# Moving POOL's arithmetic to DVE, and a new order of layer 0's second MLP half

## The chip, the cores and the metric

The kernel runs on one core of one Trainium2 chip. The metric is the device time of one execution in microseconds. The engines in the profile are PE (TensorE matmuls; PEld its weight loads), DVE (VectorE), ACT (ScalarE), POOL (GpSimd) and SP (SyncE, which issues most DMAs). Each engine works through its own list of instructions in order; an instruction starts when what it needs has been signalled.

## The reference

A two-layer backbone over 1024 latent tokens and 256 context tokens, width 1024, in float32:

```python
def modulate(h, shift, scale):
    return h * (1 + scale) + shift

def sq_relu_mlp(h, w1, w2):
    return jnp.square(jax.nn.relu(h @ w1)) @ w2

# even layer: one projection -> [bidirectional chunked GLA | GQA with QK-RMSNorm and 2-D axial rotary]
y = jnp.concatenate([y_a, y_b], axis=-1) @ w_out
# odd layer: one projection -> [bidirectional order-2 Hyena | differential attention with rotary]
y = jnp.concatenate([hyena, diff], axis=-1) @ w_out
# both: pre-RMSNorm, adaLN shift and scale, mixer (or MLP), post-RMSNorm, adaLN gate, residual add
```

The context tokens pass through layer 0 whole; of layer 1 only the latent tokens are put out. The shift, scale and gate vectors come from the conditioning vector by six projections per layer.

## The kernel before

**Matmuls in three terms.** Each float32 operand is split into a high part, rounded to PE's format, and a low part, the rest. `split` (L92) has ACT copy `hi` (L94) and then DVE or POOL subtract `lo = src - hi` (L95); its flag `pool` says which. A product is then three matmuls: hi·hi, lo·hi, hi·lo.

**Stages.** Layer 0: the in-projection, with head norms (L488) and roping (`rope`, L606: L611 multiplies on DVE, L616 and L618 multiply and add on POOL) and, in the background, `ada_halves`, which works out modulation vectors on DVE (L259, L261) and splits the sums as `ada_hl`; grouped attention, woven with Hyena's filters (`hy_filters`, whose loads `hy_m` POOL issues); GLA (lines 875 to 1047; gating at L1004 and L1008, the decayed keys at L927, the masked scores at L960); the out-projection with its norms and residuals (`post_norm`, L1050, whose last add, L1061, alternates between POOL and DVE); and the MLP. Layer 1: the in-projection with short convolutions (`cb_hi`, `cb_lo`), differential attention (L644 to L668) woven with it, Hyena's long convolution (`hy_conv`, whose loads `hm` POOL issues, whose sums L1955 to L1961 DVE does), the out-projection (`wo_hi`, `wo_lo`) and the MLP.

**The MLP's first half** (`Up`) forms the seven products of a Strassen-like scheme, in 16 blocks of the hidden width, and writes the blocks to HBM as `hid`. Its weight splits `w_lo<-up_w` are shared by POOL and DVE; the flag `by_pool` of `keep` (L1208) says which.

**The second half** (`mlp_down`, L1414) has seven products too, in the order p1, p2, p3, p5, p6, p7, p4 (`DOWN`), each summed in PSUM over 16 blocks k of the hidden width: 112 steps. A step i has three parts. `load(i)` fetches a block of activations (`dn_h`) and one or two of weights (`dn_b`; `dn_t` for those that p5, p6 and p4 share), and, where context tokens take part, `dn_c`. `prep(i + 2)` subtracts weight blocks where the product asks for it (L1477) and splits both operands into pairs (`dn_h_hi`, `dn_h_lo`, `dn_w_hi`, `dn_w_lo`), then calls `load` for a step further on. `terms` issues twelve matmuls (L1515 to L1517) into four PSUM banks, `context` six more (L1526 to L1528) in p1, p2, p3 and p5. After a product's last block `put` (L1490 to L1500) adds the banks into the accumulators `accx` and `accy`. The context's sums `accz` are complete after p5, those of the first four row tiles of latent tokens (`accx`) after p7, the other four (`accy`) after p4. `ends` is a pipeline of stages (post-norm and residual, then the next layer's norm) that the program advances in every second step of p7 and p4, the context's tiles first; the scheduler puts the context's gating on DVE before p6's last splits. The modulation vectors that are still missing run beside the steps as `bg`, at the pace of `rates`. The tuple `bufs` gives the numbers of buffers: activations, weights, context blocks, pairs; it is (5, 6, 4, 6) in layer 0.

**What sets the order.** DMAs wait in order on the queue of the engine that issues them. Names of a buffer ring make a write wait until the last reader of that buffer is done. The order of each engine's list comes from a scheduler that follows the program's order and the waits between instructions, so a change of engine for one instruction also shifts its neighbours; tables below show the lists.

Of the kernel before, what the change touches and what calls it, by code (L numbers as in the profile page):

```python
# [91 lines left out]
def split(g, hi, lo, src, pool=False):  # L92

    g.nc.scalar.activation(hi, src, ACTF.Copy)  # L94
    (g.nc.gpsimd if pool else g.nc.vector).tensor_tensor(lo, src, f(hi), op=ALU.subtract)  # L95
# [369 lines left out]
def in_proj0(g, ps, ftp, vgp):  # L465
# [12 lines left out]
    with ExitStack() as st:  # L478
# [6 lines left out]
        def head_norm(src, nh, gain):  # L485
            r = head_rstd(g, pq[0], src, nh, 64, f"rp_u{nh}")
            nc.vector.tensor_tensor(src, src, r.unsqueeze(2).to_broadcast([128, nh, 64]), op=ALU.mult)
            nc.gpsimd.tensor_tensor(src, src, gain.unsqueeze(1).to_broadcast([128, nh, 64]), op=ALU.mult)  # L488
# [117 lines left out]
def rope(g, pool, src, nh, t1, t2):  # L606
# [8 lines left out]
    for k in range(2):  # L615
        nc.gpsimd.tensor_tensor(uv[:, :, :, k], sv[:, :, :, 1 - k],  # L616
                                tv[:, :, k].unsqueeze(1).to_broadcast([128, nh, 32]), op=ALU.mult)
    nc.gpsimd.tensor_tensor(o, o, u, op=ALU.add)  # L618
# [207 lines left out]
def gla(g, st, y_put):  # L826
# [81 lines left out]
    def weights(t, b, p, la):  # L908
# [18 lines left out]
        nc.gpsimd.tensor_tensor(gate(ee), gate(ee), kb, op=ALU.mult)  # L927
# [23 lines left out]
    def inner(t, b, ee, kinT):  # L951
# [8 lines left out]
        nc.gpsimd.tensor_tensor(aT, ab[b][:, :, 0, :], ab[b][:, :, 1, :], op=ALU.add)  # L960
# [31 lines left out]
    def forward(t):  # L992
# [11 lines left out]
        nc.gpsimd.tensor_scalar(sgf, gt, -80.0, None, op0=ALU.max)  # L1004
# [3 lines left out]
        nc.gpsimd.tensor_tensor(sgf, sgf, gt, op=ALU.mult)  # L1008
# [41 lines left out]
def post_norm(g, y, x_t, gate, tmp, junk, pool=True):  # L1050
# [10 lines left out]
    (nc.gpsimd if pool else nc.vector).tensor_tensor(x_t, x_t, tmp, op=ALU.add)  # L1061
# [116 lines left out]
class Up:  # L1178
# [235 lines left out]
def mlp_down(g, layer, ap, pool, x_src, bg, rates, after, group, bufs):  # L1414
# [25 lines left out]
    raws, parts, cs, gates = {}, {}, {}, []  # L1440
# [5 lines left out]
    def load(i):  # L1446
# [3 lines left out]
        q = nc.scalar if i < 2 else nc.sync  # L1450
# [81 lines left out]
    def tiles(n):  # L1532
        return [psa(g, [128, 512], name="dn_ps", tag="dp") for _ in range(n)]
# [17 lines left out]
    ends = [done(t, zs[t]) for t in range(len(zs))] + [done(NC_T + t, xs[t]) for t in range(4)]  # L1551
    ends = pipelined(item(e) for e in ends)
# [6 lines left out]
    for i, (n, k) in enumerate(steps[:len(steps) - group]):  # L1559
# [73 lines left out]
def w_block(g, raw, pool=None, split_pairs=False):  # L1633
# [4 lines left out]
    if split_pairs:  # L1638
        h, r = (x.rearrange("p k (c d) -> p (k c) d", d=64) for x in (hi, raw))
        l = lo.rearrange("p k (c d) -> p (k c) d", d=64)  # L1640
        for x in range(2):
# [3 lines left out]
            (nc.vector if 2 > x else nc.gpsimd).tensor_tensor(l[:, :, sl], v, f(h[:, :, sl]), op=ALU.subtract)  # L1645
# [728 lines left out]
def tile_kernel(ctx, tc, ins, out):  # L2374
# [57 lines left out]
    with st:  # L2432
        with ExitStack() as s2:
            ap, pool = pool_of(s2, "acc0", "left"), pool_of(s2, "res0", "left")
            hs = {}
            with ExitStack() as sp:
# [3 lines left out]
                                (norm, hs.__setitem__), 4, (5, 6, 4, 6))  # L2440
# [150 lines left out]
```

## Time and profile before

| | us |
|---|---|
| median of three runs (lowest, highest) | 3390.24 (3385.76, 3394.58) |
| the profiled execution, and its span | 3387.06, 3385.3 |
| PE busy | 3134.7 (93%) |
| DVE busy, 4507 instructions | 2489.5 (74%) |
| ACT busy | 1538.6 (45%) |
| POOL busy, 392 instructions | 528.0 (16%) |
| mean granted clock of TensorE | 0.967 of full speed |

The times in the prediction's rows are microseconds from the span's start. The stages lie about as follows: layer 0's in-projection to 345, attention to 690, GLA and the filters to 960, out-projection to 1115, the MLP's first half to 1464 and second half to 1900; layer 1's in-projection and attention to 2400, Hyena to 2645, out-projection to 2800, and its MLP to the end.

### The profile page before, as it was taken

The numbers are of one execution on the slowest core, as the hardware profiler recorded it, in microseconds if no ns is written. First come the engines' busy times: TensorE is split into PE (matmuls) and PEld (weight loads), VectorE is DVE, ScalarE is ACT, GpSimd is POOL, SyncE is SP. The second block draws the span as 40 slices with busy tenths as digits, with TensorE's granted clock in tenths as the row PEclk, the third lists the DMA queues.
The fourth block names the chain that finished last, engine by engine and source line by source line (L and its number), as shares of the span: only waits on it lengthen the run. The fifth ranks groups of instructions, "written<-read, shape, count | busy, mean of one in ns | idle before, by whom it ended". The sixth has DMA issues, their size and how long they took to land.

```text
span 3385.3 us, 41884 instructions
## 1 busy us (share of the span) xinstructions
PE 3134.7 (93%) x13896; PEld 2405.3 (71%) x13896; DVE 2489.5 (74%) x4507; ACT 1538.6 (45%) x3150; POOL 528.0 (16%) x392
## 2 busy tenths in 40 slices
PE   8879999889987999989998899999968989999998
PEld 4766777667766788868876777766635667887886
DVE  6787767677658776766688666677778489877777
ACT  4444766554655222223345543576621352224453
POOL 0153000123222122201111112100020122210000
PEclk9999999999998999999999999999989999999999
DMA  6544111667753343378777455432344635438964
GB/s 227 154 129 147 55 40 47 178 193 228 244 199 114 132 146 131 134 255 297 240 245 241 135 167 168 116 97 74 122 142 135 226 113 168 146 137 303 314 194 161
DMA packets 344581, 566.69 MB, mean 167 GB/s; under 512 B 43329, under 2 KB 138561, under 8 KB 344236
## 3 DMA queue, kind: packets, MB, share of 16 engines
q1 hardware_dynamic: 296244, 491.19, 44.4%
q10 hardware_dynamic: 40952, 47.67, 4.1%
q0 software_dynamic: 7168, 25.17, 2.5%
q8 instruction: 109, 1.79, 0.2%
q14 instruction: 108, 0.88, 0.1%
HBM read 410.36 MB, written 153.55 MB: 167 GB/s over the span
## 4 chain that ended last, share of the span: by engine, by line
PE 63%; DVE 14%; issue 10%; DMA 7%; ACT 3%; POOL 3%; SPq 0%; ACTq 0%; POOLq 0%; DVEq 0%
PE up_ps L105 5%; PE up_ps L104 5%; PE up_ps L103 5%; PE dn_ps L1516 5%; PE dn_ps L1515 5%; PE dn_ps L1517 5%; PE s_ps L644 2%; PE up_ps L1234 1%; PE s_ps L738 1%; PE o_ps L2224 1%; DMA up_w<-in_w_mlp_in 1%; PE st_ps L758 1%; PE st_ps L759 1%; DVE ada_acc L261 1%; PE o_ps L771 1%
## 5 line engine op out<-in xcount | busy, mean ns | idle before, releaser
L1515 PE MATMUL dn_ps<-dn_w_hi,dn_h_hi 128*128 128x512 f32 x896 | 351.3, 394 | 28.2 <-DVE accy L1496 14.3
L1516 PE MATMUL dn_ps<-dn_w_lo,dn_h_hi 128*128 128x512 f32 x896 | 352.9, 394 | 5.3 <-DVE dn_w_lo L95 5.3
L1517 PE MATMUL dn_ps<-dn_w_hi,dn_h_lo 128*128 128x512 f32 x896 | 351.5, 392 | 0.0
L94 ACT ACTIVATE dn_h_hi<-dn_h 128x512 fp32r<-128x512 f32 x224 | 140.8, 629 | 279.4 <-PE dn_ps L1516 192.1
L95 POOL TENSOR_TENSOR w_lo<-up_w,w_hi 128x512 fp32r<-128x512 f32 x106 | 144.4, 1372 | 582.8 <-ACT w_hi L94 548.1
L95 DVE TENSOR_TENSOR dn_h_lo<-dn_h,dn_h_hi 128x512 fp32r<-128x512 f32 x224 | 161.9, 723 | 83.7 <-ACT dn_h_hi L94 83.3
L1515 PEld LDWEIGHTS dn_ps<-dn_w_hi,dn_h_hi 128*128 128x128 f32 x896 | 169.8, 190 | 67.7 <-DVE accy L1496 16.1
L1516 PEld LDWEIGHTS dn_ps<-dn_w_lo,dn_h_hi 128*128 128x128 f32 x896 | 170.1, 190 | 43.6 <-DVE dn_w_lo L95 8.5
L1517 PEld LDWEIGHTS dn_ps<-dn_w_hi,dn_h_lo 128*128 128x128 f32 x896 | 170.1, 190 | 35.4
L261 DVE SCALAR_TENSOR_TENSOR ada_acc<-w_ada,sc,ada_acc 128x512 f32<-128x512 f32 x224 | 169.0, 791 | 19.7 <-DMA w_ada<-in_w_ada 19.0
L94 ACT ACTIVATE s_hi<-up_w 128x512 fp32r<-128x512 f32 x128 | 79.1, 630 | 192.6 <-DVE up_w L1223 113.3
L95 DVE TENSOR_TENSOR gq_lo<-gq_p,gq_hi 128x512 fp32r<-128x512 f32 x168 | 115.4, 690 | 55.9 <-ACT gq_hi L94 54.3
L105 PE MATMUL up_ps<-t_hi,s_lo 128*128 128x512 f32 x384 | 152.3, 398 | 2.4 <-DVE s_lo L95 2.4
L104 PE MATMUL up_ps<-t_lo,s_hi 128*128 128x512 f32 x384 | 152.0, 396 | 2.8 <-DVE t_lo L95 2.8
L103 PE MATMUL up_ps<-t_hi,s_hi 128*128 128x512 f32 x384 | 152.6, 397 | 1.4 <-ACT t_hi L94 1.3
L1223 DVE TENSOR_TENSOR up_w<-up_w 128x512 f32<-128x512 f32 x128 | 94.0, 737 | 79.0 <-POOL w_lo L95 77.2
L654 DVE TENSOR_REDUCE sm_m<-s_ps 128x1 f32<-128x512 f32 (+1 forms) x192 | 110.2, 595 | 44.7 <-PE s_ps L644 43.3
L95 POOL TENSOR_TENSOR ada_hl<-ada_acc,ada_hl 128x512 fp32r<-128x512 f32 x32 | 62.3, 1958 | 510.7 <-ACT ada_hl L94 359.4
L739 DVE TENSOR_REDUCE gq_mx<-s_ps 128x1 f32<-128x256 f32 (+1 forms) x208 | 112.2, 580 | 29.1 <-PE s_ps L738 28.2
L668 ACT ACTIVATE df_p<-s_ps,sm_m 128x512 f32<-128x512 f32 (+1 forms) x192 | 116.7, 618 | 34.5 <-DVE sm_m L658 31.1
L94 ACT ACTIVATE w_hi<-up_w 128x512 fp32r<-128x512 f32 x106 | 64.7, 628 | 142.4 <-DMA up_w<-in_w_mlp_in 63.5
L761 ACT ACTIVATE gq_p<-st_ps 128x512 f32<-128x512 f32 x168 | 99.7, 597 | 61.2 <-PE st_ps L759 60.3
(499 smaller groups left out, 8906.6 us busy)
## 6 DMA issues: line engine op xcount, KB each, us to landing
dn_b<-in_w_mlp_out SPq DMA_DIRECT2D x252, 256.0 KB
w_ada<-in_w_ada SPq DMA_DIRECT2D x96, 512.0 KB
up_w<-in_w_mlp_in SPq DMA_DIRECT2D x32, 1024.0 KB
hy_m<-in_k_ff POOLq DMA_DIRECT2D x32, 512.0 KB, 5.1
dn_c<-hidc SPq DMA_DIRECT2D x64, 256.0 KB
x<-x_in SPq DMA_DIRECT2D x26, 512.0 KB
x_in<-x SPq DMA_DIRECT2D x26, 512.0 KB
cb_raw<-in_od_w_in SPq DMA_DIRECT2D x20, 512.0 KB
```

Source lines behind the costliest of these rows:

```text
L94: g.nc.scalar.activation(hi, src, ACTF.Copy)
L95: (g.nc.gpsimd if pool else g.nc.vector).tensor_tensor(lo, src, f(hi), op=ALU.subtract)
L103: nc.tensor.matmul(out, ah, bh, start=(i == 0), stop=False)
L104: nc.tensor.matmul(out, ah, bl, start=False, stop=False)
L105: nc.tensor.matmul(out, al, bh, start=False, stop=(i == n - 1))
L261: nc.vector.scalar_tensor_tensor(acc[:, s], w[:, k], sc, acc[:, s], op0=ALU.mult, op1=ALU.add)
L654: nc.vector.tensor_reduce(m[:, i:i + 1], s, axis=AX.X, op=ALU.max)
L668: g.nc.scalar.activation(d, s, ACTF.Exp, bias=m, scale=0.125, accum_out=l[:, i:i + 1])
L739: nc.vector.tensor_reduce(mx[u][:, i, j:j + 1], ps, axis=AX.X, op=ALU.max)
L1515: nc.tensor.matmul(ps, hh[:, sl], wh, start=(k == 0), stop=False)
L1516: nc.tensor.matmul(ps, hh[:, sl], wl, start=False, stop=False)
L1517: nc.tensor.matmul(ps, hl[:, sl], wh, start=False, stop=(k == nb - 1))
```

## The change

It has two parts.

**The engine of arithmetic.** Every tensor operation that POOL did moves to DVE, but for the low parts of the weights in the MLP's first halves (`w_lo<-up_w`, 106 instructions): 212 instructions, 116 of them 512 elements wide, 40 of 1024, two of 2048, and 54 of 256 or less. `split` now ignores its fifth positional argument, so that only a call that names `pool=` reaches POOL. POOL keeps these w_lo, some fills of memory, and DMA issues.

**Layer 0's second MLP half.** The first two steps' loads are issued by POOL instead of ACT; activations and weights have 8 and 9 buffers instead of 5 and 6, the pairs 4 instead of 6; the `dn_t` tiles are taken from the pool of loads at the start; the context's gate is fetched at the start of p6 and the context's ends run there, in a pipeline of their own, while the latent tokens' ends stay in p7 and p4; of the four banks of p7 two come from the context's ring (`cx`), of those of p4 one, so that three of the four are not those that the product before holds to its end (before, all came from one ring of five, `dp`).

```diff
-def split(g, hi, lo, src, pool=False):
+def split(g, hi, lo, src, _=False, pool=False):
...
-                nc.gpsimd.tensor_tensor(lo, src, f(hi), op=ALU.subtract)
+                nc.vector.tensor_tensor(lo, src, f(hi), op=ALU.subtract)
...
-            nc.gpsimd.tensor_tensor(src, src, gain.unsqueeze(1).to_broadcast([128, nh, 64]), op=ALU.mult)
+            nc.vector.tensor_tensor(src, src, gain.unsqueeze(1).to_broadcast([128, nh, 64]), op=ALU.mult)
...
-        nc.gpsimd.tensor_tensor(uv[:, :, :, k], sv[:, :, :, 1 - k],
+        nc.vector.tensor_tensor(uv[:, :, :, k], sv[:, :, :, 1 - k],
...
-    nc.gpsimd.tensor_tensor(o, o, u, op=ALU.add)
+    nc.vector.tensor_tensor(o, o, u, op=ALU.add)
...
-        nc.gpsimd.tensor_tensor(gate(ee), gate(ee), kb, op=ALU.mult)
+        nc.vector.tensor_tensor(gate(ee), gate(ee), kb, op=ALU.mult)
...
-        nc.gpsimd.tensor_scalar(sgf, gt, -80.0, None, op0=ALU.max)
+        nc.vector.tensor_scalar(sgf, gt, -80.0, None, op0=ALU.max)
...
-        nc.gpsimd.tensor_tensor(sgf, sgf, gt, op=ALU.mult)
+        nc.vector.tensor_tensor(sgf, sgf, gt, op=ALU.mult)
...
-    (nc.gpsimd if pool else nc.vector).tensor_tensor(x_t, x_t, tmp, op=ALU.add)
+    nc.vector.tensor_tensor(x_t, x_t, tmp, op=ALU.add)
...
-        split(self.g, hi, lo, src, by_pool)
+        split(self.g, hi, lo, src, pool=by_pool)
...
-    raws, parts, cs, gates = {}, {}, {}, []
+    raws, parts, gates = {}, {}, {}
+    if ctx:
+        ts = {k: rp.tile([128, 512], F32, name=f"dn_t{k}") for k in range(nb)}
...
-        q = nc.scalar if i < 2 else nc.sync
+        q = (nc.gpsimd if ctx else nc.scalar) if i < 2 else nc.sync
...
-        return [psa(g, [128, 512], name="dn_ps", tag="dp") for _ in range(n)]
+        tags = {"p7": ("dp", "cx", "cx", "dp"), "p4": ("dp", "dp", "dp", "cx")} if ctx else {}
+        return [psa(g, [128, 512], name="dn_ps", tag=tag) for tag in tags.get(n, ("dp",) * 4)]
...
-    ends = [done(t, zs[t]) for t in range(len(zs))] + [done(NC_T + t, xs[t]) for t in range(4)]
-    ends = pipelined(item(e) for e in ends)
+    ctx_ends = pipelined(item(done(t, zs[t])) for t in range(len(zs)))
+    ends = pipelined(item(done(NC_T + t, xs[t])) for t in range(4))
...
+            if n == "p6" and ctx:
+                gates.update({1: mod(g, p, layer, 5, (1,), name="gate")[0]})
             if n == "p7":
                 run(bg)
-                gates.extend(mod(g, pool, layer, 5, range(2 - layer), name="gate", tag="gate", bufs=2))
+                gates.update({0: mod(g, pool, layer, 5, (0,), name="gate", tag="gate", bufs=2)[0]})
...
+        if n == "p6" and k % 2:
+            next(ctx_ends, None)
...
-                                (norm, hs.__setitem__), 4, (5, 6, 4, 6))
+                                (norm, hs.__setitem__), 4, (8, 9, 4, 4))
```

The lists of instructions below are as they are issued, without times; a row's names are out<-in, its sizes partitions x elements, and xN stands for N like rows in a row.

ACT at the end of layer 0's first MLP half, before (`up_r`, `up_c`: the last block's context rows; `hid_0p` and `hid_1p`: the first two blocks of activations):

```order
L1237 COPY up_r<-up_ps 128x256
L94 ACTIVATE up_c<-up_r 128x256
L1452 DMA dn_h<-hid_0p_9557 128x512
L1460 DMA dn_b<-in_w_mlp_out 128x512
L1452 DMA dn_h<-hid_1p_9564 128x512
L1460 DMA dn_b<-in_w_mlp_out 128x512
L94 ACTIVATE dn_h_hi<-dn_h 128x512
L94 ACTIVATE dn_w_hi<-dn_b 128x512
```

POOL with the change, at the same place of the program:

```order
L95 TENSOR_TENSOR w_lo<-up_w,w_hi 128x512 x64
L1454 DMA dn_h<-hid_0p_9557 128x512
L1464 DMA dn_b<-in_w_mlp_out 128x512
L1454 DMA dn_h<-hid_1p_9564 128x512
L1464 DMA dn_b<-in_w_mlp_out 128x512
L1990 DMA hm<-in_k_df 128x512 x8
```

The four issues left ACT's list, where they stood between the first half's last split and the second half's first, for POOL's, where they stand behind the last of layer 0's w_lo.

DVE in layer 0's second half, before, among the splits for p6's last two steps (`accz`: the context's sums; `dn_t`: p6's weights):

```order
L95 TENSOR_TENSOR dn_w_lo<-dn_t_16147,dn_w_hi 128x512
L1060 SCALAR_TENSOR_TENSOR accz_13914<-accz_13914,rs_t,gate 128x1024
L1060 SCALAR_TENSOR_TENSOR accz_13915<-accz_13915,rs_t,gate 128x1024
L95 TENSOR_TENSOR dn_h_lo<-dn_h,dn_h_hi 128x512
L95 TENSOR_TENSOR dn_w_lo<-dn_t_16186,dn_w_hi 128x512
L1061 TENSOR_TENSOR x_in<-x_in,accz_13915 128x1024
```

DVE with the change, among the splits for p6's steps 6 and 7:

```order
L1060 SCALAR_TENSOR_TENSOR accz_13914<-accz_13914,rs_t,gate 128x1024
L95 TENSOR_TENSOR dn_h_lo<-dn_h,dn_h_hi 128x512
L1061 TENSOR_TENSOR x_in<-x_in,accz_13914 128x1024
L95 TENSOR_TENSOR dn_w_lo<-dn_t_13928,dn_w_hi 128x512
L95 TENSOR_TENSOR dn_h_lo<-dn_h,dn_h_hi 128x512
L95 TENSOR_TENSOR dn_w_lo<-dn_t_13929,dn_w_hi 128x512
```

The gating of the context's sums moved forward by some eight steps, the two tiles stand apart, and both residual adds are now in DVE's list, one of which POOL had.

POOL at the end of Hyena's convolution, before (`hm`: the transform's matrices; `wo_lo`: the out-projection's weights):

```order
L1981 DMA hm<-in_k_df 128x512 x2
L95 TENSOR_TENSOR wo_lo_23224<-wo_raw,wo_hi_23223 128x1024
L1981 DMA hm<-in_k_di 128x512
L95 TENSOR_TENSOR wo_lo_23230<-wo_raw,wo_hi_23229 128x1024
L1981 DMA hm<-in_k_di 128x512
L95 TENSOR_TENSOR wo_lo_23236<-wo_raw,wo_hi_23235 128x1024
```

DVE with the change, there (`hz`: the convolution's outputs, from PSUM):

```order
L1970 TENSOR_TENSOR hz<-y_ps,hz 128x512 x2
L95 TENSOR_TENSOR wo_lo_23224<-wo_raw,wo_hi_23223 128x1024
L95 TENSOR_TENSOR wo_lo_23230<-wo_raw,wo_hi_23229 128x1024
L1970 TENSOR_TENSOR hz<-y_ps,hz 128x512 x2
L95 TENSOR_TENSOR wo_lo_23236<-wo_raw,wo_hi_23235 128x1024
L95 TENSOR_TENSOR wo_lo_23242<-wo_raw,wo_hi_23241 128x1024
```

The eight wo_lo left their places between POOL's DMA issues for places between DVE's evacuations.

More of the change, by code (lines that the diff above doesn't have):

```diff
@@ L959, in inner @@
         aT = wk.tile([128, 4, 128], F32, name="gl_aT", tag="gl_aT")
-        nc.gpsimd.tensor_tensor(aT, ab[b][:, :, 0, :], ab[b][:, :, 1, :], op=ALU.add)
+        nc.vector.tensor_tensor(aT, ab[b][:, :, 0, :], ab[b][:, :, 1, :], op=ALU.add)
         return t, b, ee, aT
@@ L1455, in load @@
             if n == "p5" and b == "b12":
-                w = ts[k] = p.tile([128, 512], F32, name=f"dn_t{k}")
+                if not ctx:
+                    ts[k] = p.tile([128, 512], F32, name=f"dn_t{k}")
+                w = ts[k]
             else:
@@ L1565, in mlp_down @@
         if k == 0:
-            ps = tiles(4)
+            ps = tiles(n)
             if n in ("p1", "p3") and ctx:
                 cps = [psa(g, [128, 512], name="dc_ps", tag="cx") for _ in range(2)]
+            if n == "p6" and ctx:
+                gates.update({1: mod(g, p, layer, 5, (1,), name="gate")[0]})
             if n == "p7":
                 run(bg)
-                gates.extend(mod(g, pool, layer, 5, range(2 - layer), name="gate", tag="gate", bufs=2))
+                gates.update({0: mod(g, pool, layer, 5, (0,), name="gate", tag="gate", bufs=2)[0]})
         for t in range(4):
@@ L1644, in w_block @@
             nc.scalar.activation(h[:, :, sl], v, ACTF.Copy)
-            (nc.vector if 2 > x else nc.gpsimd).tensor_tensor(l[:, :, sl], v, f(h[:, :, sl]), op=ALU.subtract)
+            nc.vector.tensor_tensor(l[:, :, sl], v, f(h[:, :, sl]), op=ALU.subtract)
     else:
```

## The prediction

> **What bounds the kernel now.** I read the page's shares and its chain of waits first, then the table of windows by stage (length; PE, PEld, DVE, ACT, POOL busy; granted clock; DMA share; GB/s).
>
> ```profile
> span 3385.3 us, 41884 instructions
> PE 3134.7 (93%) x13896; PEld 2405.3 (71%) x13896; DVE 2489.5 (74%) x4507; ACT 1538.6 (45%) x3150; POOL 528.0 (16%) x392
> PE 63%; DVE 14%; issue 10%; DMA 7%; ACT 3%; POOL 3%; SPq 0%; ACTq 0%; POOLq 0%; DVEq 0%
> 85.00:345.00 260.00, 225.57 (x1120) 180.49 (x1119) 205.56 (x417) 118.18 (x270) 90.39 (x80) 0.93 0.46 142
> 960.00:1115.00 155.00, 125.45 (x552) 99.34 (x551) 124.19 (x227) 90.88 (x190) 38.95 (x21) 0.91 0.41 140
> 1464.00:1515.00 51.00, 38.56 (x164) 30.99 (x163) 34.45 (x54) 20.26 (x35) 3.37 (x2) 0.87 0.93 316
> 1780.00:1900.00 120.00, 108.00 (x458) 88.13 (x457) 95.11 (x177) 61.36 (x123) 11.18 (x4) 0.94 0.65 217
> 2120.00:2400.00 280.00, 272.10 (x1284) 200.18 (x1282) 211.59 (x510) 190.35 (x495) 24.24 (x12) 1.00 0.34 92
> 2645.00:2800.00 155.00, 133.60 (x580) 103.31 (x579) 115.80 (x207) 78.19 (x155) 30.67 (x17) 0.94 0.49 168
> ```
>
> TensorE is busy 93%, so at most 3385.3 − 3134.7 = 251 us of idle time, and what the clock loses around it, is there to win. The windows split it: in 2120–2400 (differential attention) PE has 8 us of slack and nothing on DVE or POOL can gain much; in 85–345 (layer 0's in-projection, roping) 34 us, in 960–1115 and 2645–2800 (output projections, norms) 30 and 21, at the start of layer 0's second MLP half (1464) 12 of 51, in its last products (1780) 12. In those stretches DVE is the second busiest, at 67 to 80%, and it is what the change loads further.
>
> **Part A, arithmetic from POOL to DVE: prices.** POOL's groups (count | busy us, mean ns | idle before, releaser), then the nearest groups of DVE.
>
> ```profile
> L95 POOL TENSOR_TENSOR w_lo<-up_w,w_hi 128x512 fp32r<-128x512 f32 x106 | 144.4, 1372 | 582.8 <-ACT w_hi L94 548.1 <-PE up_ps L104 34.5 <-DMA up_w<-in_w_mlp_in 0.2
> L95 POOL TENSOR_TENSOR ada_hl<-ada_acc,ada_hl 128x512 fp32r<-128x512 f32 x32 | 62.3, 1958 | 510.7 <-ACT ada_hl L94 359.4 <-DMA p<-stg 119.0 <-DMA dn_h<-hid_14p 32.2
> L616 POOL TENSOR_TENSOR rp_u<-stg,tq 128x64 f32<-128x64 f32 (+1 forms) x32 | 27.7, 884 | 10.3 <-DVE hr_ss L628 7.6 <-ACT w_hi L94 1.9 <-DVE v_st L511 0.5
> L1061 POOL TENSOR_TENSOR x_in<-x_in,y_h 128x1024 f32<-128x1024 f32 x9 | 22.1, 2458 | 103.9 <-DVE y_h L1060 80.6 <-DVE rs_t L118 16.6 <-PE tr_ps L2303 3.5
> L488 POOL TENSOR_TENSOR stg<-stg,gq_gq 128x512 f32<-128x512 f32 x10 | 20.8, 2085 | 22.9 <-DVE stg L487 16.1 <-ACT qT L549 4.9 <-ACT cols L291 1.9
> L95 POOL TENSOR_TENSOR wo_lo<-wo_raw,wo_hi 128x1024 fp32r<-128x1024 f32 x8 | 18.8, 2354 | 5.3 <-ACT wo_hi L94 5.3
> L1004 POOL TENSOR_SCALAR gl_sg<-gl_g 128x512 f32<-128x512 f32 x10 | 16.6, 1655 | 33.3 <-DMA yd<-gl_sg 14.7 <-DVE rs_t L118 10.3 <-PE kv_ps L980 8.3
> L1008 POOL TENSOR_TENSOR gl_sg<-gl_sg,gl_g 128x512 f32<-128x512 f32 x10 | 13.9, 1393 | 24.8 <-ACT gl_sg L1007 24.8
> L1875 POOL DMA_DIRECT2D hy_m<-in_k_ff x32 | 17.8, 557 | 89.4 <-PE sp_ps L105 46.6 <-PE gk_ps L898 31.3 <-PE lr_ps L893 5.2
> L95 DVE TENSOR_TENSOR gq_lo<-gq_p,gq_hi 128x512 fp32r<-128x512 f32 x168 | 115.4, 690 | 55.9 <-ACT gq_hi L94 54.3
> L95 DVE TENSOR_TENSOR wo_lo<-wo_raw,wo_hi 128x1024 fp32r<-128x1024 f32 x8 | 10.1, 1264 | 2.9 <-ACT wo_hi L94 2.9
> L656 DVE TENSOR_TENSOR sm_m<-sm_m 128x1 f32<-128x1 f32 x64 | 14.3, 223 | 1.1
> L116 DVE SCALAR_TENSOR_TENSOR rs_t<-rs_t 128x1 f32<-128x1 f32 (+3 forms) x112 | 36.7, 338 | 25.2 <-ACT rs_t L115 25.0
> L261 DVE SCALAR_TENSOR_TENSOR ada_acc<-w_ada,sc,ada_acc 128x512 f32<-128x512 f32 x224 | 169.0, 791 | 19.7 <-DMA w_ada<-in_w_ada 19.0
> ```
>
> 212 instructions move. What stays is w_lo (144.4), 64 DMA issues (64 × 0.557 = 36) and about 6 of memsets, so POOL loses 528.0 − 186 = 342 us. On DVE the 116 of width 512 cost 116 × 0.690 = 80, the 40 of 1024 cost 40 × 1.264 = 51, the two of 2048 twice 1.264, 5, and the 54 of 256 or less, of a shape without a clean row, between 0.15 (a 1-wide one, below) and 0.69; I take 0.3, the nearer end for 64 to 256 elements, 16. Sum 152 us, 137 to 173.
>
> A part of that comes back, because DVE stalls while POOL works. Two rows of the timeline (start, length):
>
> ```profile
> 2307.72 3.07 POOL L95 TENSOR_TENSOR cb_lo<-cb_raw,cb_hi 128x1024 fp32r<-128x1024 f32 x1 [34.53 <-ACT cb_hi L94]
> 2308.55 2.25 DVE L656 TENSOR_TENSOR sm_m<-sm_m 128x1 f32<-128x1 f32 x1
> 1794.84 0.16 DVE L116 SCALAR_TENSOR_TENSOR rs_t<-rs_t 128x1 f32<-128x1 f32 x1 [0.50 <-ACT rs_t L115]
> ```
>
> A one-element operation of 0.16 us lasts 2.25, until POOL's is over. By the groups: L116 112 × (0.338 − 0.16) = 20, L656 64 × 0.06 = 4, L261 224 × (0.791 − 0.690) = 23 at most; these alone are 47 us, some 30% of it due to w_lo, which stays (144 of 487 us of arithmetic). So 33 us is a floor of what the moved work cost DVE; with the other groups I estimate three times that, 100. DVE gains 152 and loses 33 to 100: **net +50 to +120 us over the span**, 1.5 to 3.5 points of its 74%.
>
> The Trainium skill ("GPSIMD Engine Reference", section 3.1) gives a ratio of 1.96 for a two-input operation on POOL; by it the moved 342 us would be 175 on DVE instead of 152, which changes no sign. The rows' ratios, 2354/1264 = 1.86 and 1958/690 = 2.84, straddle it.
>
> **Part A by stage.** What counts is POOL on the chain. In 85–345:
>
> ```profile
> by line: DVE ada_acc L261 11.8%; issue 10.4%; DMA gk<-kT 4.9%; POOL rp_u L616 4.3%; POOL rp_o L618 3.9%; DMA w_ada<-in_w_ada 3.8%; DMA w_raw<-in_ev_w_in 3.7%; POOL stg L488 3.5%; PE s_ps L738 3.0%; PE vg_ps L688 2.8%; PE vg_ps L687 2.8%; PE
> 269.53 6.01 POOL stg L488
> ```
>
> The three POOL lines are 11.7% of 260 = 30 us, and a 512-wide multiply that waits behind or beside DVE takes 6 us at worst. At DVE's prices (0.69/2.085, a third) 30 becomes 10; but the moved work queues in order behind L261, on an engine that is busy 206 of 260 us, so I book half of the 20: −10. In 960–1115 and 2645–2800 the nine x_in adds of L1061's row shorten from 2.46 to about 1.26 us, all in the chain of residual and norm that feeds the MLP: nine times 1.2 is 11, of which I book −4 in each stage. In 1965–2400 cb_lo (3.07 us in the row above) and ada_hl stop stalling the softmax, but PE is nearly full: −4. In the tail after 3290 four residual adds lose 1.2 us each: −4. GLA's four lines only lie on POOL while TensorE is fed by Hyena's filters: 0. In Hyena's end the eight wo_lo come into DVE's list among the evacuations of y_ps; each waits for ACT and a DMA (5.3 us of idle in all in its row): +3, bounds 0 and +8. Sum −23; since DVE is one in-order list in which each moved instruction now also delays its successors, I book two thirds: **A = −16**, between −40 and +20.
>
> **Part B, layer 0's second half.** Its start: POOL's last w_lo, the chain, and PE's waits:
>
> ```profile
> 1438.29 1.35 POOL L95 TENSOR_TENSOR w_lo<-up_w,w_hi 128x512 fp32r<-128x512 f32 x1 [5.71 <-ACT w_hi L94]
> 1465.97 2.04 DMA hid_15p<-up_u
> 1468.04 0.35 ACTq L1452
> 1468.42 7.48 DMA dn_b<-in_w_mlp_out
> 1475.92 0.64 ACT dn_w_hi L94
> 1476.60 0.80 PE dn_ps L1515
> PE dn_ps L1515 <- ACT dn_w_hi L94: 13.0, 2, 12.4
> PE dn_ps L1515 <- DVE accy L1496: 12.0, 2, 8.4
> ```
>
> ACT issues the first loads after its last split of the first half, when the last block's products are being written; dn_b then takes 7.48 us. On POOL the four issues stand behind w_lo only, whose last begins 30 us before ACT's first issue, and need products p1 of blocks 0 and 1, long written, and buffers that the last block's products free; I take half of that lead, 15 us, twice what dn_b needs. Then ACT splits as soon as the first half ends: if the first issue's 7.48 us and the wait before it fall away, the first matmul starts near 1467.6 instead of 1476.6: −9. The clock in 1464–1515 is 0.87, 0.13 × 51 = 6.6 us of lost speed; with a gap of 3 instead of 12 I expect a quarter back, −1.6. Step 2's loads, still on SP, have two steps of 18 matmuls (at 0.236 us by the 1780 window, 4 us each) as cover.
>
> The Trainium skill ("DMA: Bandwidth & Descriptors", Issuing engine by pattern) calls SyncE's and ScalarE's queues generally faster than GpSimd's, which speaks against this edit; with the lead, a few us more would lie under the first half, so the sum stays.
>
> At the turn from p6 to p7 (PE stops at 1796.6, goes on at 1805) three things stall DVE: the gate's DMA, POOL, and a late load.
>
> ```profile
> 1780.30 5.65 DMA gate<-mods
> 1786.05 2.48 DVE L1060 SCALAR_TENSOR_TENSOR accz<-accz,rs_t,gate 128x1024 f32<-128x1024 f32 x2 [3.23 <-DMA gate<-mods]
> 1788.44 2.88 DVE L95 TENSOR_TENSOR dn_h_lo<-dn_h,dn_h_hi 128x512 fp32r<-128x512 f32 x1
> 1803.05 0.69 DVE L1477 TENSOR_TENSOR dn_b<-dn_b 128x512 f32<-128x512 f32 x1 [2.83 <-DMA dn_b<-in_w_mlp_out]
> ```
>
> Behind these in DVE's list stand p6's last sums (L1496), which free the banks that p7 waits for: 8.4 us, and 3.6 more in the same way from p7 to p4 (the 12.0 above), at a clock of 0.94 in 1780–1900 (0.06 × 120 = 7 us). After: the gate is asked for at p6's start, the context's ends run in p6's middle, loads are 8 and 9 deep, and three of the four banks of p7, and of p4, are not those that the product before holds to its end. At best −19; hi/lo pairs are 4 instead of 6, so DVE and ACT can run only four steps (48 matmuls at 108.00/458 = 0.236 us, 11 us of PE) ahead before a late load reaches PE, and a gap may move into a product, so I take half, −9.5. **B = −20**, between −28 and −5 (if p4's gaps return elsewhere).
>
> Sum: 3387.06 (the profiled run; span 3385.3 and 1.8 around it) − 16 − 20 = 3351. The median, 3390.24, lies 3.2 above that run: **3354 us**.
>
> **Rivals.**
> - *Only B pays* (3370): A's shorter latencies are eaten by DVE's longer list. For it: DVE is already 79% busy in 85–345. Against: POOL's 30 us on that chain.
> - *Everything pays* (3323): A's −40 (all 20 of 85–345, the whole contention on the chain) and B's −27. The Trainium skill ("GPSIMD Engine Reference", section 8) says the two engines share SBUF interfaces, in conflict where DVE has two SBUF inputs; L656's row agrees. Against: w_lo stays.
> - *No change* (3388): PE's 63% of the chain closes every gap later; the gaps only move.
> - *Slower, head of line* (3410): DVE is in order, and GLA's L1004 waits for loads (14.7 us over its row's 10), L1008 for three ACT functions (24.8); wo_lo for ACT and DMA. On POOL this cost nobody; the three rows' idle time is 33 + 25 + 5 = 63 us, and two thirds of it as stalls of DVE, ahead of the sums that free PE's banks, are +40, with B's −20. It decides if more than half of those waits land in stretches where PE has no other work.
>
> **How the numbers follow.** Forecast 0.42, only B 0.24, everything 0.11, no change 0.13, slower 0.10. The forecast's own terms spread it over 3335–3372. The range for 8 in 10 cuts half of the last rival and some of the best case: 3325 to 3392. About 0.3% (10 us) can be told from no change here: faster than 3380 are the forecast, the best case and nearly all of "only B", 0.76; within, 0.14; slower, 0.10.
>
> **What would show it.** L656's mean near 0.16 and L261's near 0.7; DVE busy 2540–2610 us and POOL about 190; POOL gone from the chain of 85–345; PE's gap at the second half's start 3 to 5 us instead of 12.4, and those before p7 and p4 under 6 in all instead of 12.0. Wrong if DVE waits for ACT or DMA at moved lines while PE idles, if DVE's share of the chain grows by what POOL's falls, or if new gaps open inside p6, p7 or p4.

## The result, and the profile after

The changed kernel takes 3332.52 us (median; 3331.21 to 3334.66), the one before 3390.12 (3385.76 to 3394.58): a ratio of 0.9828, 95% interval 0.9814 to 0.9843. That is 57.6 us faster. The prediction said 36 us faster (3354, range 3325 to 3392): the right way and inside the range, but a good third too little, and, as the runs show, with the two parts weighed the wrong way round. Of the runs below, one execution of e7 took 6082.61 us at a granted clock of 0.943 (0.967 to 0.969 in the others) and is left out, so e7's time is the median of three.

The page of the changed kernel: span, busy times, chain of waits by engine.

```profile
span 3329.4 us, 41625 instructions
PE 3120.8 (94%) x13896; PEld 2401.5 (72%) x13896; DVE 2505.9 (75%) x4719; ACT 1543.1 (46%) x3150; POOL 186.9 (6%) x184
PE 73%; DVE 13%; DMA 5%; ACT 4%; issue 3%; POOL 0%; SPq 0%; ACTq 0%; DVEq 0%; POOLq 0%
```

DVE runs 212 instructions more and is busy only 2505.9 − 2489.5 = 16 us longer, not 50 to 120. POOL, down by 341 us, has left the chain. PE is busy 13.9 us less with the same 13896 matmuls, so its idle time fell by 56 − 14 = 42 us. Little of the 13.9 is the clock: the mean granted clock is 0.967 in both, which over the two spans is 112 us of lost speed before and 110 after. The trace has 1170 matmuls longer than 0.42 us before and 1109 after; why these were fewer is not settled.

DVE's groups in the changed kernel (count | busy us, mean ns | idle before):

```profile
L95 DVE TENSOR_TENSOR ada_hl<-ada_acc,ada_hl 128x512 fp32r<-128x512 f32 x32 | 21.7, 686 | 0.6 <-ACT ada_hl L94 0.4
L616 DVE TENSOR_TENSOR rp_u<-stg,tq 128x64 f32<-128x64 f32 (+1 forms) x32 | 9.2, 318 | 0.0
L1061 DVE TENSOR_TENSOR x_in<-x_in,y_h 128x1024 f32<-128x1024 f32 x18 | 21.9, 1219 | 0.1
L656 DVE TENSOR_TENSOR sm_m<-sm_m 128x1 f32<-128x1 f32 x64 | 9.9, 155 | 0.8
L116 DVE SCALAR_TENSOR_TENSOR rs_t<-rs_t 128x1 f32<-128x1 f32 (+3 forms) x112 | 16.2, 154 | 9.7 <-ACT rs_t L115 9.6
L261 DVE SCALAR_TENSOR_TENSOR ada_acc<-w_ada,sc,ada_acc 128x512 f32<-128x512 f32 x224 | 160.0, 746 | 25.0 <-DMA w_ada<-in_w_ada 24.3
```

The moved operations cost what was priced (0.686 for 512 wide, 1.219 for 1024, 0.318 for rope's), and the stalled ones shrank: L116 from 338 to 154 ns, L656 from 223 to 155, L261 from 791 to 746. If the lengths of all DVE instructions are added up, they come to 2731 us before and 2774 after, 43 more: the moved ones are 148 of the 2774, and the others became 105 shorter in all. The busy time counts the overlap of neighbours once, and so rose by 16 only. (Two rows further below show such an overlap: L259 starts at 1451.80 and lasts 0.48, and the next instruction starts at 1452.20.)

Stages of the changed kernel (length; PE, PEld, DVE, ACT, POOL busy; granted clock; DMA share; GB/s):

```profile
85.00:280.00 195.00, 171.45 (x900) 141.47 (x899) 167.35 (x429) 88.32 (x213) 0.00 (x0) 0.93 0.58 180
1442.00:1493.00 51.00, 42.96 (x180) 34.24 (x180) 32.62 (x53) 17.94 (x30) 0.00 (x0) 0.90 0.89 307
2070.00:2350.00 280.00, 271.57 (x1268) 199.99 (x1266) 210.99 (x522) 189.20 (x494) 2.13 (x4) 0.98 0.33 91
```

and the stage of the first row in the kernel before:

```profile
85.00:300.00 215.00, 181.24 (x917) 147.63 (x915) 169.66 (x348) 87.62 (x216) 90.39 (x80) 0.92 0.52 162
```

In the in-projection DVE has 81 instructions more and is busy 2 us less: what it took over (9.2 for rope's products, 7.7 for its adds, 9.7 for the gains, 8.2 for ada_hl, 35 us) is paid for the most part by stalls that ended. Its idle time fell from 45 to 28 us, and with it the stage, from 215 to 195.

The second half's start, on POOL, SP, DVE and PE of the changed kernel:

```profile
1426.23 0.58 POOL L1454 DMA_DIRECT2D dn_h<-hid_0p  x1 [8.05 <-PE up_ps L105]
...
1446.21 0.97 SPq L253 DMA_DIRECT2D w_ada<-in_w_ada  x2
...
1445.87 0.69 DVE L95 TENSOR_TENSOR dn_h_lo<-dn_h,dn_h_hi 128x512 fp32r<-128x512 f32 x1
1450.80 0.49 DVE L259 TENSOR_SCALAR ada_acc<-w_ada,sc 128x512 f32<-128x512 f32 x1 [4.24 <-DMA w_ada<-in_w_ada]
1451.20 0.69 DVE L95 TENSOR_TENSOR dn_w_lo<-dn_b,dn_w_hi 128x512 fp32r<-128x512 f32 x1
1451.80 0.48 DVE L259 TENSOR_SCALAR ada_acc<-w_ada,sc 128x512 f32<-128x512 f32 x1
1452.20 0.69 DVE L95 TENSOR_TENSOR dn_h_lo<-dn_h,dn_h_hi 128x512 fp32r<-128x512 f32 x1
...
1442.41 0.28 PE L1235 MATMUL up_ps<-ftc,w_lo 128*128 128x256 f32 x1
1446.41 1.22 PE L1519 MATMUL dn_ps<-dn_w_hi,dn_h_hi 128*128 128x512 f32 x2 [3.72 <-ACT dn_w_hi L94]
1451.94 0.80 PE L1520 MATMUL dn_ps<-dn_w_lo,dn_h_hi 128*128 128x512 f32 x1 [4.32 <-DVE dn_w_lo L95]
```

The gap of 12.4 us became two, 3.7 and 4.3. The first is as forecast. The second is new: DVE's list has an operation of the background (L259) between the two low parts of step 0, and it waits 4.24 us for a DMA that SP issues only now. The longest waits of PE in the second half:

```profile
PE dn_ps L1520 <- DVE dn_w_lo L95: 5.5, 5, 4.3
PE dn_ps L1519 <- ACT dn_w_hi L94: 3.7, 1, 3.7
```

No wait of PE for DVE's accy is left (one of 0.4 us, for ACT's, is): the gaps before p7 and p4 are gone.

### The profile page after: what moved, and what is told of

It is laid out like the page before. It is cut to its first block, busy times and chain, and to the rows that moved or that the text cites. A ratio compares the mean times of both kernels' runs of the same rounds, so it can differ in the third digit from the quotient of the medians.

```text
span 3329.4 us, 41625 instructions
## 1 busy us (share of the span) xinstructions
PE 3120.8 (94%) x13896; PEld 2401.5 (72%) x13896; DVE 2505.9 (75%) x4719; ACT 1543.1 (46%) x3150; POOL 186.9 (6%) x184
## 4 chain that ended last, share of the span: by engine, by line
PE 73%; DVE 13%; DMA 5%; ACT 4%; issue 3%; POOL 0%; SPq 0%; ACTq 0%; DVEq 0%; POOLq 0%
PE dn_ps L1520 6%; PE dn_ps L1521 6%; PE up_ps L105 6%; PE dn_ps L1519 6%; PE up_ps L103 6%; PE up_ps L104 6%; PE s_ps L644 2%; PE o_ps L2233 2%; DVE ada_acc L261 2%; PE fa_ps L2004 1%; PE up_ps L1234 1%; PE y_ps L2004 1%; PE s_ps L738 1%; PE pj_ps L104 1%; PE pj_ps L103 1%
## 5 line engine op out<-in xcount | busy, mean ns | idle before, releaser
L95 DVE TENSOR_TENSOR dn_h_lo<-dn_h,dn_h_hi 128x512 fp32r<-128x512 f32 x224 | 153.9, 687 | 74.2 <-ACT dn_h_hi L94 68.3
L261 DVE SCALAR_TENSOR_TENSOR ada_acc<-w_ada,sc,ada_acc 128x512 f32<-128x512 f32 x224 | 160.0, 746 | 25.0 <-DMA w_ada<-in_w_ada 24.3
L95 DVE TENSOR_TENSOR s_lo<-up_w,s_hi 128x512 fp32r<-128x512 f32 x128 | 94.6, 741 | 38.1 <-ACT s_hi L94 36.5
```

The costliest lines, as they stand in the source:

```text
L261: nc.vector.scalar_tensor_tensor(acc[:, s], w[:, k], sc, acc[:, s], op0=ALU.mult, op1=ALU.add)
```

## The experiments

All times stand beside runs of the kernel before on the same chip; the intervals are those of the ratio to it. The table gives the progress of the same matmuls in the traces, in us from the span's start, and against the kernel before:

| | before | change | e7 engine alone | e8 order alone | e10 one line | e9 shadow |
|---|---|---|---|---|---|---|
| first score of attention (s_ps) | 298.3 | −20.7 | −19.8 | −1.4 | −0.8 | +9.8 |
| first of the out-projection (op_ps) | 945.6 | −13.5 | −12.4 | −0.3 | −0.1 | +17.8 |
| end of layer 0's first half (up_ps) | 1464.2 | −21.5 | −21.8 | +0.9 | −6.3 | +8.0 |
| first context matmul of the second half (dc_ps) | 1481.1 | −25.3 | −21.9 | −0.4 | −5.8 | +6.8 |
| end of layer 0's second half (dn_ps) | 1899.9 | −41.2 | −32.3 | −6.7 | −9.9 | −6.6 |
| last score of layer 1's attention (s_ps) | 2450.3 | −52.3 | −44.1 | −10.5 | −13.6 | −17.1 |
| end of layer 1's first half (up_ps) | 3057.7 | −51.8 | −43.5 | −8.0 | −17.5 | −18.5 |
| span | 3385.3 | −55.9 | −46.5 | −5.8 | −21.2 | −22.3 |

One profile each; where nothing differs, two executions drift apart by some us in a stage, so differences of 3 us or less in the table are not read as effects.

**e1, e2: the buffer counts.** Both edits exchanged only the four counts and not the function, so they are not the two parts that their expectations speak of (e7 and e8 are).

e1 against the changed kernel; e2 is the reverse edit on the kernel before:

```diff
-                                (norm, hs.__setitem__), 4, (8, 9, 4, 4))
+                                (norm, hs.__setitem__), 4, (5, 6, 4, 6))
```

> The change without the new order of layer 0's second MLP half: only the 212 instructions move from POOL to DVE. By the cumulative times of the same matmuls in the two traces, that half (start, turns between products) gave 20 us of the 57.6, the rest 36 to 38. Theory (the two parts add up): 3390 - 37 = 3353, within 5. Rival (they help each other: it was POOL's residual add that stalled DVE at the turn from p6 to p7, so the engine change alone also heals that gap): 3343 or less, with the gap before p7 under 4 us instead of 8.4.

> The kernel before with the new order of layer 0's second MLP half alone; all of POOL's arithmetic stays on POOL. Theory (parts add up): 3390 - 20 = 3370, within 5. Rival (POOL's adds beside the context's ends still stall DVE in p6): 3380 or more. A second rival, that the loads issued on POOL now stand behind POOL's arithmetic: none is left in its list there, so the start should gain the same 4 us.

Measured: e1 3332.74 us (0.9821, 0.9803 to 0.9839), the change's own time; e2 3392.49 (1.0005, 0.9994 to 1.0016), that of before. Neither deeper loads nor fewer pairs move the time in either kernel; what the new order brings comes from its other edits.

**e7, e8: the two parts apart.** e7 is the changed kernel with the whole `mlp_down` of before, e8 the kernel before with that of the change. e7 against the changed kernel, cut to its core; e8 is the reverse:

```diff
-        q = (nc.gpsimd if ctx else nc.scalar) if i < 2 else nc.sync
+        q = nc.scalar if i < 2 else nc.sync
...
-    ctx_ends = pipelined(item(done(t, zs[t])) for t in range(len(zs)))
-    ends = pipelined(item(done(NC_T + t, xs[t])) for t in range(4))
+    ends = [done(t, zs[t]) for t in range(len(zs))] + [done(NC_T + t, xs[t]) for t in range(4)]
+    ends = pipelined(item(e) for e in ends)
...
-                                (norm, hs.__setitem__), 4, (8, 9, 4, 4))
+                                (norm, hs.__setitem__), 4, (5, 6, 4, 6))
```

> Only the 212 instructions move from POOL to DVE; the whole function of the second MLP half, its buffers too, is that of the kernel before (the run e1 had exchanged the buffer counts only). Theory (the parts add up, and the 20 us between the first half's end and the next layer are the new order's): 3353, between 3348 and 3358, with the gaps before p7 and p4 (8.4 and 3.6) there again. Rival (POOL's add and its stall of DVE made those gaps): 3343 or less, both gaps together under 5.

> Only the new order of layer 0's second MLP half, with its buffers; all arithmetic that POOL had stays there. Theory (the parts add up): 3370, between 3365 and 3375, with start gap 8 us in two pieces and no gap before p7 and p4. Rival (POOL's adds x_in and its ada_hl still stall DVE, whose lists now carry the context's ends in p6): 3380 or more.

Measured: e7 3336.75 us (0.9851, 0.9831 to 0.9870), e8 3381.11 (0.9982, 0.9972 to 0.9991). Both times are the rivals' (e8's by 1 us), and so are e7's two gaps, 3.0 us together. By the ratios the parts nearly add up (50 + 6 of 58), but not as either theory priced them: the engine change is worth some 50 us, the new order 6 to 8, by e8's interval 3 to 9. PE's waits in the second half, of e7 and then of e8:

```profile
PE dn_ps L1515 <- ACT dn_w_hi L94: 13.3, 3, 12.0
PE dn_ps L1515 <- DVE accy L1496: 3.0, 3, 2.2
```

```profile
PE dn_ps L1520 <- DVE dn_w_lo L95: 9.4, 8, 6.3
PE dn_ps L1519 <- ACT dn_w_hi L94: 6.0, 2, 3.7
```

In e7 the start's gap is still 12.0, but the wait for accy before p7 and p4 fell from 12.0 to 3.0 with the old order: the 8.4 before p7 are gone, 2.2 of the 3.6 before p4 are left. In e8 PE waits for no accy either, so either part closes the gap before p7; but one of 2.3 us opens inside p7 (the rest of the second row). And in e8 the start's gap is 3.7 + 6.3 = 10 us, the second piece behind DVE's L259 again, which waits 6.2 us for w_ada there; by the first context matmul (table) e8 has gained nothing.

**e10: one line.** Only the residual add of `post_norm`, 18 instructions.

```diff
-    (nc.gpsimd if pool else nc.vector).tensor_tensor(x_t, x_t, tmp, op=ALU.add)
+    nc.vector.tensor_tensor(x_t, x_t, tmp, op=ALU.add)
```

> The kernel before with one line moved: the residual add of post_norm (18 instructions, 46 us on POOL). In e7 the gap before p7 fell from 8.4 to nothing without the new order. Theory (it was this add on POOL, which DVE's next split stood beside for 2.9 us and which ACT awaited for 9 us, that delayed the sums before p7): the gaps before p7 and p4 together fall from 12.0 to under 5, the out-projections give 4 to 8, the time 3372 to 3380. Rival (the gate's DMA and the late dn_b made the gaps, and e7's gain there comes from ada_hl and the rest): both gaps stay over 9, the time 3383 to 3388.

Measured: 3369.76 us (0.9940, 0.9925 to 0.9956), 21 us faster, more than the theory's 3372 to 3380. PE's waits in its second half:

```profile
PE dn_ps L1515 <- ACT dn_w_hi L94: 14.3, 3, 11.9
PE dn_ps L1515 <- DVE accy L1496: 6.7, 3, 5.2
```

The wait for accy is nearly halved, 6.7 instead of 12.0, over the theory's 5 and under the rival's 9: POOL's adds made a part of it, the rest comes from elsewhere. By the table the line also gives 6 us in layer 0's out-projection, 4 in layer 1's and 4 at the end. In the kernel before ACT stood behind these adds:

```profile
ACT po_t L328 <- POOL x_in L1061: 15.2, 8, 4.6
ACT accz L328 <- POOL x_in L1061: 9.1, 1, 9.1
```

In e10 it still stands 7.0 us behind the add to accz, now on DVE, so those 9.1 were only in part POOL's. How the 21 us divide between shorter waits of ACT and stalls of DVE that ended is not separated.

**e5: three lines of the in-projection.**

```diff
-            nc.gpsimd.tensor_tensor(src, src, gain.unsqueeze(1).to_broadcast([128, nh, 64]), op=ALU.mult)
+            nc.vector.tensor_tensor(src, src, gain.unsqueeze(1).to_broadcast([128, nh, 64]), op=ALU.mult)
...
-        nc.gpsimd.tensor_tensor(uv[:, :, :, k], sv[:, :, :, 1 - k],
+        nc.vector.tensor_tensor(uv[:, :, :, k], sv[:, :, :, 1 - k],
...
-    nc.gpsimd.tensor_tensor(o, o, u, op=ALU.add)
+    nc.vector.tensor_tensor(o, o, u, op=ALU.add)
```

> The kernel before with only three lines moved to DVE: the head norms' gain and rope's two (58 instructions, POOL 74 us, 30 us of the chain in the in-projection); ada_hl and all else stay on POOL. Theory (the chain's rows say which operations matter): 12 to 17 us, 3373 to 3378. Rival (the gain of the stage came from POOL falling silent altogether, ada_hl too): under 6 us, 3384 or more.

Measured: 3379.88 us (0.9956, 0.9941 to 0.9971), 11 us faster, a little short of the theory's 12 to 17 and clear of the rival's 6. The first score comes 17.4 us earlier, against 20.7 in the change: the chain's three POOL lines carry that stage's gain, ada_hl little of it. Of the 17 some 3 are given back while attention is woven. In the profiled execution, the slowest of the five, 8 more are lost after the second half's start, where this run changed nothing; why is not settled.

**e3, e9: POOL works again, for nobody.** Both are the changed kernel, and POOL repeats the widths of the moved work of the in-projection on a scratch tile. In e3 a one-column read of the result paces it; in e9 a one-column copy that DVE makes into a tile of its own.

```diff
+def shadow(g, x, w):
...
+    s = g.shade[:, 0:w]
+    p = g.shadep.tile([128, 1], F32, name="pace", bufs=96)
+    g.nc.vector.tensor_copy(p, x[:, 0:1])
+    g.nc.gpsimd.tensor_tensor(s[:, 0:1], p, p, op=ALU.add)
+    g.nc.gpsimd.tensor_tensor(s, s, s, op=ALU.subtract)
...
+                shadow(g, f(hl[:, 1]), 512)
...
+            shadow(g, src, nh * 64)
...
+    for k in range(2):
+        shadow(g, u, nh * 32)
...
+    shadow(g, o, nh * 64)
```

This is e9; e3 has no `p`, and POOL reads `x[:, 0:1]` itself.

> The changed kernel, and in layer 0's in-projection POOL does again what it did before, but on a scratch tile that nobody reads: after each moved head norm, rope step and ada_hl a one-column operation that follows the result, and then one of the same width. The results of the kernel don't wait for any of it. Theory (contention: DVE stalls while POOL runs, and that was a third to a half of the 17 us gained in this stage): DVE's groups L116, L117 and L261 are long again there, DVE's busy time rises by 20 to 30 us, the time by 6 to 12, to 3339 to 3345. Rival (latency: it was the moved operations themselves that were long on the chain): no more than 3 us, 3332 to 3336, whatever DVE's busy time does.

> The changed kernel, and POOL repeats the widths of the moved work in layer 0's in-projection on a scratch tile, as in e3, but it is paced by 80 one-column copies on DVE into tiles that are never written again, so no buffer of the kernel waits for POOL (in e3, ACT and DVE stood 36 us behind POOL's reads of their buffers). The copies cost DVE some 80 x 0.06 to 0.16 = 5 to 13 us. Theory (contention of the two engines is a term of its own): DVE's busy time up by 25 to 40 us, the time up by 8 to 15, 3340 to 3348. Rival (what hurts is that others wait for POOL's results and buffers; the stalls of DVE alone hide behind its other work): up by no more than 5, 3332 to 3338.

Measured: e3 3376.87 us (0.9953, 0.9937 to 0.9969), 44 us slower than the change; e9 3362.41 (0.9917, 0.9896 to 0.9938), 30 us slower. Both are far over what contention was expected to cost. e3 doesn't tell the causes apart, since its reads hold buffers that other engines then wait for:

```profile
ACT hr_sq L645 <- POOL shade L99: 19.6, 10, 3.5
...
DVE rp_o L627 <- POOL shade L99: 16.0, 7, 3.4
```

e9 has no such wait. Its window of the in-projection, one group of DVE, one of the copies, and POOL's:

```profile
85.00:310.00 225.00, 178.87 (x898) 144.51 (x897) 198.72 (x507) 89.58 (x213) 110.81 (x160) 0.88 0.51 156
```

```profile
L274 DVE SCALAR_TENSOR_TENSOR ada_acc<-w_ada,sc,ada_acc 128x512 f32<-128x512 f32 x84 | 69.2, 850 | 2.3 <-DMA w_ada<-in_w_ada 2.3
...
L100 DVE COPY pace<-stg 128x1 f32<-128x1 f32 x20 | 2.9, 144 | 0.1
```

```profile
L102 POOL TENSOR_TENSOR shade<-shade 128x512 f32<-128x512 f32 (+3 forms) x80 | 73.6, 920 | 6.3
L101 POOL TENSOR_TENSOR shade<-pace 128x1 f32<-128x1 f32 x80 | 37.2, 465 | 106.8 <-DVE pace L100 98.2 <-DVE rs_t L130 3.7
```

DVE is busy 198.7 − 167.4 = 31.4 us longer, the first score comes 30.5 us later, the whole kernel takes 30 us more: in this run each microsecond of DVE in this stage is one of the kernel. The 80 copies at 0.144 are at most 11.5 of the 31; the rest, some 20, is stalls beside 111 us of POOL. So contention is a term of its own, and the run agrees with a stage that DVE bounds (its idle time there is 26 us, in the change 28); no run loads DVE there without POOL. Nor does e9 say how much of the stage's 20.7 us was contention: POOL is busier than it was in the kernel before (110.8 against 90.4 us), and more than the whole gain is lost.

**e4: GLA's four lines back on POOL**, on the changed kernel.

```diff
-        nc.vector.tensor_tensor(gate(ee), gate(ee), kb, op=ALU.mult)
+        nc.gpsimd.tensor_tensor(gate(ee), gate(ee), kb, op=ALU.mult)
...
-        nc.vector.tensor_tensor(aT, ab[b][:, :, 0, :], ab[b][:, :, 1, :], op=ALU.add)
+        nc.gpsimd.tensor_tensor(aT, ab[b][:, :, 0, :], ab[b][:, :, 1, :], op=ALU.add)
...
-        nc.vector.tensor_scalar(sgf, gt, -80.0, None, op0=ALU.max)
+        nc.gpsimd.tensor_scalar(sgf, gt, -80.0, None, op0=ALU.max)
...
-        nc.vector.tensor_tensor(sgf, sgf, gt, op=ALU.mult)
+        nc.gpsimd.tensor_tensor(sgf, sgf, gt, op=ALU.mult)
```

> The changed kernel with GLA's four lines (decayed keys, masked scores, both steps of the gating; 40 instructions) back on POOL. Between 600 and 860 us the changed kernel lost 4 us against the one before. Theory (those 4 us are DVE standing in order behind loads and exponentials of these lines): 3328 to 3330, faster than the change. Rival (they come from the filters' own order, or POOL's stalls cost as much): 3331 to 3340.

Measured: 3330.60 us (0.9829, 0.9813 to 0.9845): no difference from the change that can be measured. In its trace the out-projection begins 17.0 us earlier than in the kernel before, against 13.5 in the change, so the order of DVE does cost some 3 us in GLA; at the end 1 is left. The other runs agree: from attention's last score to the out-projection it is 333 to 336 us in all seven kernels that have these lines on POOL, and 337 to 342 in all seven that have them on DVE.

**e11, e12: the start's second gap.** POOL also issues the background's first two loads; e12 adds e4's edit.

```diff
-def ada_halves(g, pool, chunks, lag=1):
+def ada_halves(g, pool, chunks, lag=1, early=0):
...
-                nc.sync.dma_start(out=w, in_=g.i["w_ada"][layer, k2 * 256:(k2 + 1) * 256, cs].rearrange(
+                q, early = (nc.gpsimd if early else nc.sync), max(0, early - 1)
+                q.dma_start(out=w, in_=g.i["w_ada"][layer, k2 * 256:(k2 + 1) * 256, cs].rearrange(
...
-                bg = ada_halves(g, pool, [(0, 5), (1, 1), (1, 0)] + ADA[0:1])
+                bg = ada_halves(g, pool, [(0, 5), (1, 1), (1, 0)] + ADA[0:1], early=2)
```

> The changed kernel; POOL also issues the first two loads of w_ada for the modulation that runs beside layer 0's second MLP half, behind its four issues. In the changed kernel DVE waits 4.24 us for the first of them (L259) with the low part of step 0's weights behind it. Theory (that wait is the second piece of the gap at the start, 4.3 us): the piece goes, 3328 to 3330. Rival (the loads collide with those of the first steps, or the gap moves to step 2, whose loads are issued late): 3331 to 3335.

> e11 with GLA's four lines back on POOL (as in e4, whose stage from 600 to 860 us was 3 us shorter than the change's). Theory (the two gains add up): 3325 to 3329. Rival (GLA's 3 us are given back in the out-projection and e11's don't come): 3330 to 3334.

Measured: e11 3336.17 us (0.9836, 0.9818 to 0.9854), e12 3337.33 (0.9836, 0.9820 to 0.9852): no gain, and e11 and e12 stand 4 to 5 us above the change, within the intervals. In e11's profiled execution, the slowest of its four (3326.28 to 3340.18), DVE's wait for w_ada is gone, but the gap at the start is one of 10.2 us, and on ACT a split for a later product (dx_hi, p5) now stands ahead of step 0's:

```profile
1450.51 0.63 ACT L94 ACTIVATE dx_hi<-dn_t 128x512 fp32r<-128x512 f32 x1 [5.90 <-DMA dn_t<-in_w_mlp_out]
1451.05 0.61 ACT L94 ACTIVATE dn_h_hi<-dn_h 128x512 fp32r<-128x512 f32 x1
```

Moving two loads made the scheduler put another instruction there that waits for a load. What a start without either would give was not tried.

**e13: the last arithmetic off POOL too.**

```diff
-        split(self.g, hi, lo, src, pool=by_pool)
+        split(self.g, hi, lo, src)
```

> The changed kernel with the last arithmetic of POOL, the 106 w_lo (144.9 us on POOL), on DVE too (106 x 0.69 = 73 us). Theory (in the first halves PE is 99% busy, so neither DVE's load nor its stalls beside w_lo reach the end but in their first 100 us, where DVE is the chain): 3329 to 3338. Rival (what DVE loses beside w_lo, some 40 us, is worth as much as what it lost beside the moved work): 3320 to 3328.

Measured: 3332.40 us (0.9828, 0.9815 to 0.9842), the change's time. Its page:

```profile
PE 3122.4 (94%) x13896; PEld 2402.6 (72%) x13896; DVE 2518.5 (76%) x4825; ACT 1545.7 (46%) x3150; POOL 42.0 (1%) x78
```

106 instructions more on DVE, 73 us by their price, and DVE is busy only 13 us longer; but neither the stalls that end nor the load reach the time, which agrees with the theory that PE is full there. No run beat the change by more than its interval.

## Why the prediction was right or wrong

**What bounds the kernel: right.** The gain came from the idle time that the windows showed, 42 of 251 us, with 14 of PE's busy time. The full stages gave nothing: against the kernel before, the lead of the change stays within 1 us from dc_ps to the end of p5, and within 0.1 us in the first halves from 1162 and 2823 us (of the kernel before) on.

**Prices on DVE: right.** 152 us for 212 instructions, and 148 by their groups after. The range's lower end, 137, is a slip: 54 × 0.15 is 8, which makes 144.

**Stalls: the estimate of 100 right, the overlap missing.** The working booked 33 to 100 us as what DVE gets back. The lengths of the instructions that did not move fell by 105, so the guess of three times the floor was good. But the net of +50 to +120 sets the 152 and the stalls against each other as if instructions ran end to end. In summed lengths the net is +43; of that another 27 are overlaps that the busy time counts once, hence +16.

**Part A, −16 forecast, −50 measured (e7): the step that failed.** Three errors add up in it.
- The terms of the stages. Forecast and e7, by the table: in-projection −10 and −19.8 (of which 4 are given back in attention); GLA 0 and +4; layer 0's out-projection, with the first half behind it, −4 and −9.4; from layer 0's end to the end of layer 1's attention −4 and −11.8; Hyena +3 and −1; layer 1's out-projection −4 and −3, the start of the first half behind it 0 and +5; the tail −4 and −3. "I book half of the 20" was wrong for the in-projection: DVE's load there did not rise at all (169.7 to 167.4 us), so the shorter operations cost no queue, and all 20 arrived.
- "Two thirds" (of 23, booked as 16), the discount for an in-order list. What e7 loses, some 13 us (attention 4, GLA 4, the start of layer 1's first half 5), is a fifth of what it gains, not a third, and only for GLA is it shown that the order of DVE makes it (e4, some 3 us). e13 shows 106 more instructions at no cost where PE is full.
- A term was missing: the second half of layer 0's MLP, −10.5 in e7, of which 8.4 are the gap before p7. The sum has thirteen of POOL's 18 residual adds, nine and the tail's four; the five of this half stand nowhere in it. The rows quoted for it (accz, then a dn_h_lo of 2.88 us, then late sums) were read as a matter of the gate and of the order, and booked under B. The 2.88 us stood beside POOL's add, and ACT waited 9.1 us for the same add.

**Part B, −20 forecast, −6 to −8 measured (e8; e7 against the change).** The first issues on POOL did what was said: they ran 16 us before the first half's last matmul, and PE stands 3.7 us before step 0. But step 0 needs two low parts, and between them stands L259, so by the table the start gained 4 us (in e8 1) and not 10.6. The turns' −9.5 is real, but not B's alone: e8 has 6 there, and with A already there 5 are left (−15.9 in the change from dc_ps to the half's end, −10.4 in e7). The buffers and pairs, named as B's risk, did nothing (e1, e2).

**The sum.** −36 for −58: the two errors have opposite signs, and B's overestimate hid a part of A's underestimate. That the sum came as near as it did was luck, not a working that held.

**The rivals.** "Everything pays" (3323, 0.11) came nearer than the forecast (3354): A reached even more than its −40, B did not. "Only B pays" is refuted by e7, where A alone gives 50, and by e8, where B alone gives 6 to 8 and not 20. "Head of line" is real in GLA's lines, with 3 us, and at the start of layer 1's first half, where PE waits 2.9 us for uh_lo, now on DVE, and 0.7 before. L259 at the second half's start, 4 us, is of the same kind, but it is no moved instruction: e8 has it too, so the new order put it there. The rival needed two thirds of 63 us to decide. "No change" fell with the first figure.

**What would show it.** L656 at 155 ns, POOL at 187 us and off the chain, the gaps before p7 and p4 gone: as named. The gap at the start, named as 3 to 5 us, is 3.7 and then 4.3. L261 fell to 746 only. DVE's busy time of 2506 was below the 2540 to 2610 named, for the reason above.

## What to carry to other kernels

When work moves between two engines that stall each other, price three things apart: its own duration there, the stalls that end (here 105 us for 148 of work; with the overlaps the load rose by a tenth of the price), and who waited for it, ACT as well as PE. A gap that is explained by order may be made by a slow instruction beside it; look which engine the neighbours waited for before booking the gap to an edit. And the edit with the largest effect per instruction can be small: 18 adds in a chain of residual and norm were worth 21 us, 106 splits in a full stage nothing.

## What the runs showed of the hardware that was not expected

POOL's work costs DVE even where nobody waits for it: 111 us of it, on a tile of its own, made DVE some 20 us longer in e9 and the kernel 30 with the copies. And the same operation on POOL takes very different times. In the kernel before:

```profile
L95 POOL TENSOR_TENSOR ada_hl<-ada_acc,ada_hl x32: 1262/1540/9990, 119.5 to 3134.5; 128x512 fp32r<-128x512 f32 x32
```

The three numbers are the shortest, the median and the longest, in ns. On DVE the same 32 take 677 to 695 in the changed kernel. Two-input instructions of DVE ran beside POOL's three longest ones, of 3.4, 5.2 and 10.0 us, for nearly all of their time; but they ran beside some of the short ones too, so what decides is not shown.

The Trainium skill ("GPSIMD Engine Reference", section 3.1) has POOL at 1.96 times DVE's duration for a two-input add 2048 wide. The rows here agree for 1024 wide, 2458/1219 = 2.02 for the residual add. For ada_hl, 512 wide, the means give 1958/686 = 2.85, which is not the width: the shortest give 1262/677 = 1.86, and w_lo, 512 wide as well, has a mean of 1372 on POOL. For rope's short products the means give 884/318 = 2.78, the shortest ones, 64 wide, 342/216 = 1.58. The largest ratio is that of a one-input operation, GLA's L1004, 512 wide: 1655/422 = 3.92.
